# Sliding attention: TensorE's order by hand, value matmuls of both groups in pairs, modulation once a block

## Chip, cores and metric

The kernel runs on one core of a Trainium2 chip. The metric is the device time of one execution in microseconds (us). It is a whole transformer block in float32; the change touches one stage of it, 223 us of 2976.9.

## What is computed there

Group A of the token mixers is an attention over a window with a sink: 1024 queries in 8 blocks of 128, 8 query heads in 2 groups that share keys and values (width 64), a band of 384 keys around each block (256 at the two ends, and masked to a distance of 128), 256 context keys that every query sees, and one sink logit a head that takes part in the softmax and has no value.

```
def gqa_sink_attend(qb, keys, vals, bias, sink_g):
    s = jnp.einsum('bqkgd,bskd->bkgqs', qb, keys, preferred_element_type=jnp.float32) * (DH_A ** -0.5)
    if bias is not None:
        s = s + bias
    b, q = qb.shape[0], qb.shape[1]
    s_sink = jnp.broadcast_to(sink_g.astype(jnp.float32)[None, :, :, None, None], (b, KV_A, G_A, q, 1))
    p = jax.nn.softmax(jnp.concatenate([s, s_sink], axis=-1), axis=-1)[..., :-1]
    o = jnp.einsum('bkgqs,bskd->bqkgd', p.astype(vals.dtype), vals)
    return o.reshape(b, q, H_A * DH_A)
...
def modulate(h, shift, scale):
    return h * (1 + scale) + shift
```

The same stage also computes the rest of the modulation: a vector times the matrix `w_mod`, whose later columns are shift, scale and gate of the parts behind the attention. It needs nothing of the attention and is there to fill TensorE.

## The kernel before

`phase_window` (L466) loops over the 8 query blocks. `win_scores` (L499) does four heads of one group. For each head TensorE writes into one of two score buffers (`big`, two banks of PSUM each): the queries against the band's keys in two matmuls (`ks`, `kl`: the keys' high and low part), the mask as one matmul of 128 columns for each end of the band, the context keys in two matmuls, and the sink in one of two columns. VectorE then takes the negative maximum (L520), ScalarE the exponential with its sum (L522), and after four heads VectorE the four reciprocals (L525) and the scaling of the four P by them (L527).

`win_pv` (L530) does the second half for the block before. For each key tile of 128 (three of the band and two of the context; two and two at the ends) and each group it transposes the four heads' P into one bank (`t0` or `t1` in turn, L44), copies that to `PT` in SBUF (L542 on ScalarE, L544 on VectorE for one in three), and multiplies it by the values, 64 columns of the array for each group, into the accumulator `po`. Matmuls and transposes are recorded at the lines of the helpers `mm` (L41) and `tp` (L44). At the block's end ScalarE copies `po` to `oT` (L547).

`mods` is a generator over `mod_slab` (L133), for two column ranges s = 1, 2 with 16 slabs each. A slab is a load of 512 KB on SyncE's queue into `wmod` (three buffers) and four matmuls of 32 columns into four strips of one accumulator, which TensorE can run side by side. Behind a range's last slab GpSimd has cleared and loaded `bmod`, VectorE adds it (`mrows`, L154), and SyncE stores the rows (`modd`). Four slabs are asked for after each block, and at block 5 the text asks for `w_q_up`, which the next stage (`phase_up`, L549) needs: three loads of 384 KB into `wraw` (two buffers), split by a cast on ScalarE (L59) and a subtraction on VectorE (L62) into `Vb`.

Except where a block is marked with `manual_schedule`, a scheduler in the build sets the order of each engine's instructions. In this stage it does so on all engines: the text's order says what is asked for, not what stands where. It puts the loads of `w_q_up` to the front, and value matmuls, transposes and modulation between the scores as their inputs come free. An engine works its list in order; a wait holds all that is behind it.

Of the kernel before, what the change touches and what calls it, by code (L numbers as in the profile page):

```python
# [6 lines left out]
F32 = mybir.dt.float32  # L7
F32R = mybir.dt.float32r
I32 = mybir.dt.int32
U32 = mybir.dt.uint32  # L10
AF = mybir.ActivationFunctionType
ALU = mybir.AluOpType
AX = mybir.AxisListType
# [20 lines left out]
class Build:  # L34
# [205 lines left out]
    def pool(self, name, side="left", **kw):  # L240
        return self.tc.tile_pool(name=name, bufs=1, side=side, reuse_waits="tile", **kw)
# [224 lines left out]
    def phase_window(self, mods):  # L466
        nc, tc, I = self.nc, self.tc, self.I
        with self.pool("wa", "right") as wa:
            qs, ks, kl = self.qs, self.ks, self.kl
            identr, mask, ones, sink = self.win_consts  # L470
            pend = None
            for b in range(8):
                u = self.win_block(wa, b)
                self.win_scores(wa, u, 0, qs, ks, kl, identr, mask, ones, sink)
                if pend:
                    self.win_pv(wa, pend)
                self.win_scores(wa, u, 1, qs, ks, kl, identr, mask, ones, sink)
                for _ in range(4):
                    next(mods, None)
                if b == 5:  # L480
                    wq = self.vb.tile([128, 5120], F32R, name="Vb")
                    self.wq = [(wq[:, k * 1536:k * 1536 + 768], wq[:, k * 1536 + 768:k * 1536 + 1536]) for k in range(3)]
                    for k in range(3):
                        raw = wa.tile([128, 768], F32, name="wraw", bufs=2)
                        nc.sync.dma_start(raw, I["w_q_up"][k * 128:(k + 1) * 128])
                        self.split(*self.wq[k], raw)
                pend = u
            self.win_pv(wa, pend)
            for _ in mods:
                pass  # L490

    def win_block(self, wa, b):
        k0 = max(b - 1, 0)
        nb = min(b + 1, 7) - k0 + 1
        sm = self.sm
        return dict(b=b, k0=k0, nb=nb, P=[], nm=sm.tile([128, 8], F32, name="nm"),
                    sm=sm.tile([128, 8], F32, name="mmx4"))

    def win_scores(self, wa, u, g, qs, ks, kl, identr, mask, ones, sink):  # L499
        nc = self.nc  # L500
        b, k0, nb, nm, sm = u["b"], u["k0"], u["nb"], u["nm"], u["sm"]
        bw = nb * 128
        W = bw + 256
        c0 = 512 - bw
        P = []
        for h in range(g * 4, g * 4 + 4):
            ps = self.big()
            band, ctx = ps[:, c0:512], ps[:, 512:768]
            q = qs[:, h, b * 128:(b + 1) * 128]
            kb = slice(256 + k0 * 128, 256 + k0 * 128 + bw)  # L510
            self.mm(band, q, ks[:, g, kb], True, False)
            self.mm(band, q, kl[:, g, kb], False, False)
            if b:
                self.mm(ps[:, c0:c0 + 128], identr, mask[:, 0], False, b == 7)
            if b < 7:
                self.mm(ps[:, 384:512], identr, mask[:, 1], False, True)
            self.mm(ctx, q, ks[:, g, 0:256], True, False)
            self.mm(ctx, q, kl[:, g, 0:256], False, True)
            self.mm(ps[:, 768:770], ones, sink[:, h], True, True)
            nc.vector.reduce_max(nm[:, h:h + 1], ps[:, c0:770], axis=AX.X, negate=True)  # L520
            p = wa.tile([128, 656], F32, name="P", bufs=12)
            nc.scalar.activation(p[:, :W + 2], ps[:, c0:770], AF.Exp, bias=nm[:, h:h + 1], accum_out=sm[:, h:h + 1])  # L522
            P.append(p)
        ri = self.sm.tile([128, 8], F32, name="ri")[:, :4]
        nc.vector.reciprocal(ri, sm[:, g * 4:g * 4 + 4])  # L525
        for j in range(4):
            nc.vector.tensor_scalar_mul(P[j][:, :W], P[j][:, :W], ri[:, j:j + 1])  # L527
        u["P"] += P

    def win_pv(self, wa, u):  # L530
        nc = self.nc
        b, k0, nb, P = u["b"], u["k0"], u["nb"], u["P"]
        po = self.pt(3)
        kts = [2 + k0 + i for i in range(nb)] + [0, 1]
        for i, vt in enumerate(kts):
            for g in range(2):
                pt = self.pa(0, 2)
                for j in range(4):
                    self.tp(pt[:, j * 128:(j + 1) * 128], P[g * 4 + j][:, i * 128:(i + 1) * 128])
                PT = wa.tile([128, 512], F32, name="PT", bufs=5)  # L540
                if (i + g) % 3:
                    nc.scalar.copy(PT, pt)  # L542
                else:
                    nc.vector.tensor_copy(PT, pt)  # L544
                self.mm(po[g * 64:(g + 1) * 64], self.Va[:, vt, g * 64:(g + 1) * 64], PT,
                        i == 0, i == len(kts) - 1)
        nc.scalar.copy(self.oT[:, 0:4, b * 128:(b + 1) * 128], po.rearrange("p (j q) -> p j q", j=4))  # L547

    def phase_up(self):  # L549
# [1024 lines left out]
    def band_pv(self, bp, m, b, k0, nk, P):  # L1574
# [5 lines left out]
        while i < nk:  # L1580
            n2 = min(2, nk - i)
            pt = self.pa(0, 2)
            for kk in range(n2):
                for e in range(2):
                    c = kk * 256 + e * 128
                    self.tp(pt[:, c:c + 128], P[e][:, (i + kk) * 128:(i + kk + 1) * 128])
            PT = bp.tile([128, 512], F32, name="bPT", bufs=3)
            nc.scalar.copy(PT[:, :n2 * 256], pt[:, :n2 * 256])
            for kk in range(n2):
                kt = (k0 // 128) + i + kk  # L1590
                for e in range(2):
                    c = kk * 256 + e * 128
                    h = 2 * m + e
                    self.mm(po[e * 64:(e + 1) * 64], self.vb2[:, kt, h * 64:(h + 1) * 64], PT[:, c:c + 128],
                            i + kk == 0, i + kk == nk - 1)
# [214 lines left out]
    def build(self):  # L1810
        nc, tc, I = self.nc, self.tc, self.I

        pool = self.opool
        with ExitStack() as es:
            self.consts(es)
            self.dp = es.enter_context(tc.tile_pool(name="dp", bufs=1, space=DRAM))
            ek, self.cp1 = pool("cp1")
            self.krp = self.cp1
            self.modd = self.dp.tile([1, 4096], F32, name="modd")
            ehp, self.hp = pool("hp", "right")  # L1820
            ewp, self.wp = pool("wp", "right")
            self.phase_win()
            ewp.close()
            ehp.close()
            er, otp = pool("otp", "right")
            self.oT = otp.tile([128, 8, 1024], F32, name="oT")
            evb, self.vb = pool("vb", "right")
            emd, md = pool("md")

            def mods():  # L1830
                for s in (1, 2):
                    yield from self.mod_slab(md, s, self.pt(2), 3)
            self.phase_window(mods())
            emd.close()
            self.eq.close()
            self.ev.close()
            eu, self.uo = pool("uo", "right")
            self.phase_up()
            self.phase_mla()
            self.e1.close()  # L1840
            self.dbg("oT", self.oT)
            self.emk.close()
            em, self.rp = pool("rp")
            self.gf = self.rp.tile([128, 1024], F32, name="gf")
            self.phase_wout()
            eu.close()
            evb.close()
            er.close()
            self.phase_router()
            self.phase_moe()  # L1850
            self.dbg("xacc", self.xacc)
            em.close()
            ek.close()

            eh, self.hp = pool("hp2", "right")
            eb, self.bp = pool("bp")
            self.phase2_win()
            eh.close()
            for nm in ("bg", "qkvz"):
                self.dbg(nm, getattr(self, nm))  # L1860
            er, self.br = pool("br", "right")
            self.phase2_mix()
            self.dbg("oad", self.oad)
            self.ebpr.close()
            self.epre.close()
            eb.close()
            em, self.mp = pool("mp")
            e2, self.b2 = pool("b2")
            self.phase2_branch()
# [111 lines left out]
```

## Time and profile before

| | us |
|---|---|
| median of 3 runs | 2976.04 (2974.82 to 2976.28) |
| the profiled execution | 2978.69 |
| its span | 2976.9 |
| mean granted TensorE clock | 0.969 |
| first scores of the stage | 193.3 |
| first matmul of the next stage | 416.4 |

The span runs from the first instruction to the last; the profiled execution's time has another 1.8 us around it. In the rows below, PE is TensorE's matmuls, PEld its weight loads, DVE VectorE, ACT ScalarE, POOL GpSimd and SP SyncE. `t<-PT,Va` are value matmuls, `t<-wmod,ct` modulation, `t<-ident,P` transposes, `big<-...` scores. Matmuls of TensorE overlap their neighbours, so the time that one costs is the distance to the start of the next.

### The profile page before, as it was taken

What the parts mean: (1) busy time and instruction counts of PE and PEld (TensorE: products, weight loads), DVE (VectorE), ACT (ScalarE), POOL (GpSimd) and SP (SyncE); (2) the same over time, 40 slices, a digit from 0 to 9 for tenths busy, and PEclk for the clock granted to TensorE, in tenths of its full rate; (3) what the DMA queues carried; (4) which work ended last, traced back from release to release, by engine and by line L of the source; (5) the groups of instructions that cost most, each with busy time, mean ns of one, the idle gap of its engine ahead of it and who ended that gap; (6) DMA issues with size and microseconds to landing.
All of it is one profiled execution on the core that took longest, in us unless ns stands there. A gap on an engine that the chain in (4) does not pass through costs nothing. (4 is left out here: it accounts for less than half of the span.)

```text
span 2976.9 us, 36533 instructions
## 1 busy us (share of the span) xinstructions
PE 2770.0 (93%) x14180; PEld 2190.2 (74%) x14180; DVE 1774.3 (60%) x2651; ACT 1132.6 (38%) x1756; POOL 657.9 (22%) x654
## 2 busy tenths in 40 slices
PE   6999989889984999789999899999999999999997
PEld 4885556555663777578889788877898888888886
DVE  3655557777667999766437234375555445445455
ACT  4544454344324676553322223454133222222223
POOL 1000014343424887522121232030000000000000
PEclk8999999999987999899999999999999999999999
DMA  6123210001446999712453544312522111111111
GB/s 220 41 62 102 86 57 1 1 1 32 144 146 239 359 376 366 253 61 85 131 186 112 193 144 145 103 44 92 164 86 85 51 55 50 43 51 49 43 36 57
DMA packets 179981, 338.75 MB, mean 114 GB/s; under 512 B 17576, under 2 KB 104488, under 8 KB 177504
## 3 DMA queue, kind: packets, MB, share of 16 engines
q1 hardware_dynamic: 161408, 270.13, 27.2%
q0 software_dynamic: 18400, 66.28, 6.8%
q8 instruction: 112, 1.84, 0.3%
q14 instruction: 61, 0.50, 0.1%
HBM read 282.88 MB, written 53.49 MB: 113 GB/s over the span
## 5 line engine op out<-in xcount | busy, mean ns | idle before, releaser
L62 DVE TENSOR_TENSOR mlo<-mraw,mhi 128x2048 fp32r<-128x2048 f32 x63 | 222.5, 3558 | 9.3 <-ACT mhi L59 9.3
L41 PE MATMUL big<-hhi,wuhi 128*128 128x512 f32 x672 | 212.3, 393 | 0.0
L41 PE MATMUL big<-hhi,whi 128*128 128x512 f32 x656 | 210.4, 399 | 0.0
L41 PE MATMUL big<-hhi,wulo 128*128 128x512 f32 x672 | 209.5, 391 | 0.0
L41 PE MATMUL big<-hlo,wuhi 128*128 128x512 f32 x672 | 209.3, 391 | 0.0
L41 PE MATMUL big<-hlo,whi 128*128 128x512 f32 x656 | 208.5, 396 | 0.0
L41 PE MATMUL big<-hhi,wlo 128*128 128x512 f32 x656 | 207.6, 395 | 0.0
L59 ACT CAST mhi<-mraw 128x2048 fp32r<-128x2048 f32 x96 | 181.5, 1913 | 54.7 <-PE big L41 28.4
L62 POOL TENSOR_TENSOR mlo<-mraw,mhi 128x2048 fp32r<-128x2048 f32 x33 | 165.2, 5012 | 72.4 <-ACT mhi L59 68.9
L1785 DVE TENSOR_TENSOR xs<-xs,t 128x512 f32<-128x512 f32 x176 | 118.0, 686 | 83.3 <-PE t L41 83.1
L1802 POOL TENSOR_TENSOR wuraw<-wuraw,nf 128x1024 f32<-128x1024 f32 x2 | 5.2, 2622 | 723.7 <-ACT rst L100 719.0
L1744 DVE SCALAR_TENSOR_TENSOR cacc<-big,cols,cacc 128x1023 f32<-128x1023 f32 (+2 forms) x90 | 113.1, 1257 | 78.5 <-ACT cacc L1740 76.9
L62 DVE TENSOR_TENSOR wlo<-wraw,whi 128x512 fp32r<-128x512 f32 (+5 forms) x124 | 78.8, 644 | 123.8 <-ACT whi L59 122.2
L41 PEld LDWEIGHTS big<-hlo,wuhi 128*128 128x128 f32 x672 | 126.1, 188 | 28.7
L41 PEld LDWEIGHTS big<-hhi,wuhi 128*128 128x128 f32 x672 | 126.2, 188 | 27.3
L41 PEld LDWEIGHTS big<-hhi,wulo 128*128 128x128 f32 x672 | 126.2, 188 | 27.1
L782 ACT ACTIVATE P<-t 128x512 f32<-128x512 f32 x160 | 95.0, 598 | 134.2 <-PE t L41 132.9
L41 PEld LDWEIGHTS big<-hlo,whi 128*128 128x128 f32 x656 | 122.8, 189 | 26.3
L41 PEld LDWEIGHTS big<-hhi,wlo 128*128 128x128 f32 x656 | 122.8, 189 | 26.1
L41 PE MATMUL t<-wdhi,ah 128*128 128x512 f32 x352 | 137.4, 390 | 1.5 <-ACT ah L59 1.1
L41 PEld LDWEIGHTS big<-hhi,whi 128*128 128x128 f32 x656 | 121.0, 189 | 23.7
L41 PE MATMUL t<-wdlo,ah 128*128 128x512 f32 x352 | 137.3, 390 | 0.0
(606 smaller groups left out, 6931.4 us busy)
## 6 DMA issues: line engine op xcount, KB each, us to landing
mraw<-in_w_gate SPq DMA_DIRECT2D x32, 1024.0 KB, 12.6
mraw<-in_w_up SPq DMA_DIRECT2D x32, 1024.0 KB, 13.1
mraw<-in_w_down SPq DMA_DIRECT2D x32, 1024.0 KB, 9.8
wmod<-in_w_mod SPq DMA_DIRECT2D x48, 512.0 KB, 4.1
wuraw<-in_w_up SPq DMA_DIRECT2D x42, 512.0 KB, 3.9
wraw<-in_w2a SPq DMA_DIRECT2D x72, 256.0 KB, 2.8
wdraw<-in_w_down SPq DMA_DIRECT2D x22, 512.0 KB, 3.2
gxd<-gx POOLq DMA_DIRECT2D x8, 1024.0 KB, 4.7
```

The source lines that it names most:

```text
L41: self.nc.tensor.matmul(out, lhsT, rhs, start=start, stop=stop)
L59: nc.scalar.copy(hi, src)
L62: (nc.vector if lo_eng == "dve" else nc.gpsimd).tensor_sub(lo, src, hi.bitcast(F32))
L782: nc.scalar.activation(P, ps, AF.Exp, scale=self.sc_mla)
L1744: nc.vector.scalar_tensor_tensor(t[:, b:c + w], ps[:, b - tap:c + w - tap], self.col("conv_f", (2 - tap) * 44 + m), t[:, b:c + w], op0=ALU ...
L1785: nc.vector.tensor_add(xs[:, t, cs], xs[:, t, cs], ps)
L1802: nc.gpsimd.tensor_mul(y, y, nf)
```

## The change

TensorE's instructions of the stage now stand in the order of the text (`manual_schedule`). A head is a call of `win_scores`; after each one `win_pv`, now a generator, gives two steps of the block before: `turn` (four transposes and the copy to `PT` for one tile and group) or `both` (the value matmuls of both groups for one tile). The four slabs of modulation come after head 7, ahead of that block's last pair of value matmuls. The two mask matmuls of a block with both ends become one over two strips of 128 columns, ahead of `kl`, and the sink goes ahead of the context. Reciprocals are taken for two heads at a time; the even head is scaled on VectorE, the odd one on GpSimd. `P` gets 14 buffers (12 before), `PT` 4 (5), `wmod` 4 (3). `w_q_up` comes in nine pieces of 128x256 in one buffer (three of 128x768 in two).

```diff
@@ phase_window
+            with tc.manual_schedule(engines={mybir.EngineType.PE}):
+                for b in range(8):
+                    u = self.win_block(wa, b)
+                    if b == 5:
...
+                        for k in range(3):
+                            for c in range(0, 768, 256):
+                                raw = wa.tile([128, 256], F32, name="wraw")
+                                nc.sync.dma_start(raw, I["w_q_up"][k * 128:(k + 1) * 128, c:c + 256])
+                                self.split(*[w[:, c:c + 256] for w in self.wq[k]], raw)
+                    pv = self.win_pv(wa, pend) if pend else iter(())
+                    for h in range(8):
+                        self.win_scores(wa, u, h, qs, ks, kl, identr, mask, ones, sink)
+                        if h == 7:
+                            for _ in range(4):
+                                next(mods, None)
+                        for _ in range(2):
+                            next(pv, None)
+                    pend = u
+                for _ in mods:
+                    pass
+                for _ in self.win_pv(wa, pend):
+                    pass
@@ win_scores
+        self.mm(band, q, ks[:, g, kb], True, False)
+        if nb == 3:
+            self.mm(band.rearrange("p (a b) -> p a b", a=3)[:, 0:3:2], identr, mask, False, False)
+        elif b:
+            self.mm(ps[:, c0:c0 + 128], identr, mask[:, 0], False, False)
+        else:
+            self.mm(ps[:, 384:512], identr, mask[:, 1], False, False)
+        self.mm(band, q, kl[:, g, kb], False, True)
+        self.mm(ps[:, 768:770], ones, sink[:, h], True, True)
+        self.mm(ctx, q, ks[:, g, 0:256], True, False)
+        self.mm(ctx, q, kl[:, g, 0:256], False, True)
...
+        p = wa.tile([128, 656], F32, name="P", bufs=14)
...
+        if h % 2:
+            ri = self.sm.tile([128, 8], F32, name="ri", bufs=4)[:, :2]
+            nc.vector.reciprocal(ri, sm[:, h - 1:h + 1])
+            nc.vector.tensor_scalar_mul(u["P"][h - 1][:, :W], u["P"][h - 1][:, :W], ri[:, 0:1])
+            nc.gpsimd.tensor_scalar_mul(p[:, :W], p[:, :W], ri[:, 1:2])
@@ win_pv
+        def turn(i, g):
+            pt = self.pa(0, 2)
+            for j in range(4):
+                self.tp(pt[:, j * 128:(j + 1) * 128], P[g * 4 + j][:, i * 128:(i + 1) * 128])
+            t = PT[i, g] = wa.tile([128, 512], F32, name="PT", bufs=4)
+            if (i + g) % 3:
+                nc.scalar.copy(t, pt)
+            else:
+                nc.vector.tensor_copy(t, pt)
+
+        def both(i):
             for g in range(2):
...
+                self.mm(po[g * 64:(g + 1) * 64], self.Va[:, kts[i], g * 64:(g + 1) * 64], PT.pop((i, g)),
                         i == 0, i == len(kts) - 1)
+        turn(0, 0)
+        yield
+        for i in range(len(kts)):
+            turn(i, 1)
+            yield
+            if i + 1 < len(kts):
+                turn(i + 1, 0)
+                yield
+            both(i)
+            if i + 1 < len(kts):
+                yield
@@ mods
-                    yield from self.mod_slab(md, s, self.pt(2), 3)
+                    yield from self.mod_slab(md, s, self.pt(2), 4)
```

TensorE inside a block, between two heads' scores (`t_...<-PT,Va` value matmul, `t_...<-ident,P` transposes of one tile and group, `big<-` scores). Before:

```order
L44 MATMUL t_2509<-ident,P 128x128 x4
L41 MATMUL t_2484<-PT,Va 64x512 x2
L44 MATMUL t_2517<-ident,P 128x128 x4
L44 MATMUL t_2525<-ident,P 128x128 x4
L41 MATMUL big<-ks,qs 128x384
L41 MATMUL big<-kl,qs 128x384
L41 MATMUL t_2484<-PT,Va 64x512
L44 MATMUL t_2533<-ident,P 128x128 x4
L41 MATMUL big<-mask,identr 128x128 x2
L41 MATMUL big<-ks,qs 128x256
L41 MATMUL big<-kl,qs 128x256
```

After:

```order
L44 MATMUL t_2471<-ident,P 128x128 x4
L41 MATMUL t_2442<-PT,Va 64x512 x2
L41 MATMUL big<-ks,qs 128x384
L41 MATMUL big<-mask,identr 128x2x128
L41 MATMUL big<-kl,qs 128x384
L41 MATMUL big<-sink,onesr 128x2
L41 MATMUL big<-ks,qs 128x256
L41 MATMUL big<-kl,qs 128x256
L44 MATMUL t_2490<-ident,P 128x128 x4
L44 MATMUL t_2497<-ident,P 128x128 x4
```

The value matmuls, which stood alone or in twos and sometimes inside a head's scores, now stand in twos between whole heads, with at least one head between a pair and the transposes that it needs last.

TensorE around the modulation of the same block (`t_2007` or `t_2013` is its accumulator). Before:

```order
L41 MATMUL t_2484<-PT,Va 64x512
L44 MATMUL t_2493<-ident,P 128x128 x4
L44 MATMUL t_2501<-ident,P 128x128 x4
L41 MATMUL t_2007<-wmod,ct 32x256 x4
L41 MATMUL big<-ks,qs 128x384
```

After:

```order
L41 MATMUL big<-ks,qs 128x256
L41 MATMUL big<-kl,qs 128x256
L41 MATMUL t_2013<-wmod,ct 32x256 x16
L41 MATMUL t_2442<-PT,Va 64x512 x2
L41 MATMUL big<-ks,qs 128x384
L41 MATMUL big<-mask,identr 128x2x128
```

Before, a block's modulation is spread in groups of 1 to 12 matmuls over it; now all 16 stand in one place, ahead of the block's last two value matmuls.

SyncE's loads and ScalarE's work at the start of the stage (`Vb<-wraw` is the cast of a piece of `w_q_up`). SyncE before:

```order
L139 DMA wmod<-in_w_mod 128x4x256 x3
L485 DMA wraw<-in_w_q_up 128x768 x2
L139 DMA wmod<-in_w_mod 128x4x256 x3
L485 DMA wraw<-in_w_q_up 128x768
L139 DMA wmod<-in_w_mod 128x4x256 x12
```

SyncE after:

```order
L139 DMA wmod<-in_w_mod 128x4x256 x4
L482 DMA wraw<-in_w_q_up 128x256 x3
L139 DMA wmod<-in_w_mod 128x4x256 x4
L482 DMA wraw<-in_w_q_up 128x256 x2
L139 DMA wmod<-in_w_mod 128x4x256 x4
L482 DMA wraw<-in_w_q_up 128x256 x3
L139 DMA wmod<-in_w_mod 128x4x256 x4
L482 DMA wraw<-in_w_q_up 128x256
L139 DMA wmod<-in_w_mod 128x4x256 x2
```

ScalarE before:

```order
L522 ACTIVATE P,mmx_1914<-big,nm 128x514 x2
L59 CAST Vb<-wraw 128x768 x2
L522 ACTIVATE P,mmx_1914<-big,nm 128x514 x5
L59 CAST Vb<-wraw 128x768
L522 ACTIVATE P,mmx_1914<-big,nm 128x514
L522 ACTIVATE P,mmx_2033<-big,nm 128x642
```

ScalarE after:

```order
L529 ACTIVATE P,mmx_1916<-big,nm 128x514 x2
L59 CAST Vb<-wraw 128x256
L529 ACTIVATE P,mmx_1916<-big,nm 128x514 x2
L59 CAST Vb<-wraw 128x256
L529 ACTIVATE P,mmx_1916<-big,nm 128x514 x3
L59 CAST Vb<-wraw 128x256
L529 ACTIVATE P,mmx_1916<-big,nm 128x514
L529 ACTIVATE P,mmx_2039<-big,nm 128x642
```

The loads of `w_q_up` go between groups of four slabs, and the casts, all three in the first block before, are spread over several blocks.

## Rows read from the trace of the kernel before

**Rows 1.** The page, part 1: busy us of each engine (share of the span), xinstructions.

```profile
PE 2770.0 (93%) x14180; PEld 2190.2 (74%) x14180; DVE 1774.3 (60%) x2651; ACT 1132.6 (38%) x1756; POOL 657.9 (22%) x654
```

**Rows 2.** Windows: length, busy us of PE PEld DVE ACT POOL (xinstructions), clock, DMA.

```profile
193.00:221.00 28.00, 23.82 (x147) 22.64 (x149) 5.87 (x20) 9.57 (x24) 2.48 (x5) 0.94 0.24 78
221.00:245.00 24.00, 22.20 (x160) 13.83 (x150) 15.92 (x30) 14.55 (x32) 0.00 (x0) 1.00 0.58 178
...
320.00:345.00 25.00, 24.47 (x149) 14.49 (x148) 12.32 (x22) 11.06 (x25) 0.00 (x0) 1.00 0.27 85
...
395.00:416.00 21.00, 17.83 (x92) 8.66 (x89) 6.51 (x12) 8.30 (x18) 0.56 (x1) 1.00 0.28 101
```

**Rows 3.** Timeline of PE, fourth block: start, busy us, operation, xrecords [idle before <-releaser].

```profile
269.77 1.58 PE L41 MATMUL t<-PT,Va 128*64 128x512 f32 x4
271.28 1.09 PE L44 MATMUL t<-ident,P 128*128 128x128 f32 x8
...
274.90 0.16 PE L41 MATMUL big<-sink,onesr 128*128 128x2 f32 x1
274.92 0.42 PE L41 MATMUL big<-ks,qs 128*128 128x384 f32 x1
...
282.93 1.09 PE L44 MATMUL t<-ident,P 128*128 128x128 f32 x8
283.95 0.64 PE L41 MATMUL t<-wmod,ct 128*32 128x256 f32 x8
284.52 0.44 PE L41 MATMUL big<-ks,qs 128*128 128x384 f32 x1
...
284.97 0.34 PE L41 MATMUL big<-mask,identr 128*128 128x128 f32 x2
285.14 0.33 PE L41 MATMUL big<-ks,qs 128*128 128x256 f32 x1
...
285.43 0.17 PE L41 MATMUL big<-sink,onesr 128*128 128x2 f32 x1
285.52 1.07 PE L41 MATMUL t<-PT,Va 128*64 128x512 f32 x2
286.53 0.66 PE L44 MATMUL t<-ident,P 128*128 128x128 f32 x4
287.11 1.87 PE L41 MATMUL t<-PT,Va 128*64 128x512 f32 x4
288.92 1.09 PE L44 MATMUL t<-ident,P 128*128 128x128 f32 x8
289.77 0.42 PE L41 MATMUL big<-ks,qs 128*128 128x384 f32 x1
```

**Rows 4.** Timeline of PE, start of the modulation.

```profile
220.42 1.07 PE L41 MATMUL t<-wmod,ct 128*32 128x256 f32 x16 [1.50 <-ACT cqT L405]
```

**Rows 5.** Lines, 193 to 416 us: xcount | busy us, mean ns | idle before, releasers.

```profile
L41 PE MATMUL t<-PT,Va 128*64 128x512 f32 x152 | 69.7, 617 | 4.3 <-ACT PT L542 2.9 <-DVE ri L525 0.9 <-DVE PT L544 0.4
...
L520 DVE TENSOR_REDUCE nm<-big 128x1 f32<-128x642 f32 x48 | 39.1, 824 | 54.1 <-PE big L41 53.2
L522 ACT ACTIVATE P<-big,nm 128x642 f32<-128x642 f32 x48 | 38.3, 799 | 36.1 <-DVE nm L520 28.7 <-PE t L44 7.1
...
L41 PE MATMUL t<-wmod,ct 128*32 128x256 f32 x256 | 25.2, 389 | 3.1 <-DMA wmod<-in_w_mod 1.6 <-ACT cqT L405 1.5
...
L527 DVE TENSOR_SCALAR P<-P,ri 128x640 f32<-128x640 f32 x48 | 23.3, 548 | 0.2
```

**Rows 6.** Lines, GpSimd, whole span.

```profile
L787 POOL TENSOR_TENSOR acc<-P 128x512 f32<-128x512 f32 x8 | 10.3, 1286 | 19.1 <-ACT P L782 19.0
```

**Rows 7.** Tile bP, another softmax's P: duration ns min/median/max, first and last start.

```profile
L1570 DVE TENSOR_SCALAR bP<-bP,mm x64: 285/553/2630, 1905.7 to 2048.6; 128x640 f32<-128x640 f32 x32, 128x128 f32<-128x128 f32 x8, 128x256 f32<-128x256 f32 x8, 128x384 f32<-128x384 f32 x8
```

**Rows 8.** The page's DMA issues: xcount, KB each, median us to landing.

```profile
wmod<-in_w_mod SPq DMA_DIRECT2D x48, 512.0 KB, 4.1
...
wraw<-in_w_q_up SPq DMA_DIRECT2D x3, 384.0 KB, 8.2
```

More of the change, by code (lines that the diff above doesn't have):

```diff
@@ L471, in phase_window @@
             pend = None
[L472 to L490, printed above, removed]
+            with tc.manual_schedule(engines={mybir.EngineType.PE}):
+                for b in range(8):
+                    u = self.win_block(wa, b)
+                    if b == 5:
+                        wq = self.vb.tile([128, 5120], F32R, name="Vb")
+                        self.wq = [(wq[:, k * 1536:k * 1536 + 768], wq[:, k * 1536 + 768:k * 1536 + 1536])
+                                   for k in range(3)]
+                        for k in range(3):
[16 more added lines that the diff above has]
+                    pass
     def win_block(self, wa, b):
@@ L497, in win_block, with win_scores @@
                     sm=sm.tile([128, 8], F32, name="mmx4"))
-    def win_scores(self, wa, u, g, qs, ks, kl, identr, mask, ones, sink):
+    def win_scores(self, wa, u, h, qs, ks, kl, identr, mask, ones, sink):
         nc = self.nc
@@ L504, in win_scores @@
         c0 = 512 - bw
[L505 to L528, printed above, removed]
+        g = h // 4
+        ps = self.big()
+        band, ctx = ps[:, c0:512], ps[:, 512:768]
+        q = qs[:, h, b * 128:(b + 1) * 128]
+        kb = slice(256 + k0 * 128, 256 + k0 * 128 + bw)
+        self.mm(band, q, ks[:, g, kb], True, False)
@@ new lines, in win_scores @@
+        nc.vector.reduce_max(nm[:, h:h + 1], ps[:, c0:770], axis=AX.X, negate=True)
+        p = wa.tile([128, 656], F32, name="P", bufs=14)
+        nc.scalar.activation(p[:, :W + 2], ps[:, c0:770], AF.Exp, bias=nm[:, h:h + 1], accum_out=sm[:, h:h + 1])
+        u["P"].append(p)
+        if h % 2:
[3 more added lines that the diff above has]
+            nc.gpsimd.tensor_scalar_mul(p[:, :W], p[:, :W], ri[:, 1:2])
@@ L534, in win_pv @@
         kts = [2 + k0 + i for i in range(nb)] + [0, 1]
-        for i, vt in enumerate(kts):
-            for g in range(2):
[L537 to L545, printed above, removed]
-                        i == 0, i == len(kts) - 1)
+        PT = {}
+        def turn(i, g):
[8 more added lines that the diff above has]
+        def both(i):
+            for g in range(2):
+                self.mm(po[g * 64:(g + 1) * 64], self.Va[:, kts[i], g * 64:(g + 1) * 64], PT.pop((i, g)),
+                        i == 0, i == len(kts) - 1)
+        turn(0, 0)
[9 more added lines that the diff above has]
+                yield
         nc.scalar.copy(self.oT[:, 0:4, b * 128:(b + 1) * 128], po.rearrange("p (j q) -> p j q", j=4))
```

## The prediction, as it was made before the result

> **What bounds the kernel now.** I read the engines' shares first: TensorE is busy 93% of the span [rows 1]. So the stage that the diff touches, the sliding attention, was cut into stretches next [rows 2]. Inside a block TensorE is busy 24.47 of 25 us at clock 1.00, VectorE 12.32 and ScalarE 11.06, GpSimd nothing: there TensorE's own work sets the pace, and the others have half of the time to spare. Two stretches differ: the first block (22.20 of 24) and the last one, which has no scores of a next block to fill with (17.83 of 21).
>
> "Busy" hides how well TensorE is used, so the third view is its own sequence. There I read the distance from one start to the next, not the durations, since neighbours overlap. (Each value or modulation matmul leaves two records, so x2 is one value matmul, x8 one slab of four.) A value matmul alone takes 285.52 to 286.53, 1.01 us; two together, one for each group, 269.77 to 271.28, 1.51 us, so .75 each [rows 3]. One round of modulation (four matmuls of 32 columns side by side) takes 283.95 to 284.52, .57 us; two rounds in one group are busy 1.07 where one is busy .64 [rows 3, 4], so a further round costs .43, and .14 falls on each group whatever its size. The time that can be had is therefore in how TensorE's work is grouped, not in its waits: those before the value matmuls are 4.3 us in the whole stage and before the modulation 3.1 [rows 5].
>
> **The change, part by part.** All in us of the profiled execution, which took 2978.69; that is 2.65 above the median of 2976.04, so the forecast for the median is 2.65 below the sum.
>
> *Value matmuls.* The orders of the two programs give 32 alone and 22 pairs before, 38 pairs after. 32 x 1.01 + 22 x 1.51 = 65.5 becomes 38 x 1.51 = 57.4: **-8.1**. TensorE is the bound here, so all of it is on the path.
>
> *Modulation.* Before, 128 matmuls stand in 28 groups of 1 to 12, 43 rounds when each group is rounded up to fours; after, 8 groups of 16, 32 rounds. 43 x .43 + 28 x .14 = 22.4 becomes 32 x .43 + 8 x .14 = 14.9: **-7.5**. Four slabs in four buffers must be there at a block's end; they are loaded during the block before, some 20 us ahead, so I cost the loads at nothing. If that cover failed it would show as a wait like the 1.6 us that the modulation row has now [rows 5].
>
> *Mask.* Two matmuls become one of the same columns: .17 for the two (284.97 to 285.14) [rows 3]. One can cost between .085 and .17: 0 to -4.1 over 48 heads; I take .05 off each, **-2.4**.
>
> *Changes of kind of work.* Eight transposes before a modulation group take 1.02 (282.93 to 283.95), before scores .85 (288.92 to 289.77): .17 more. The order loses all 17 such places and gains 8 from transposes to a value matmul, for which I take the same .17. From the sink to a value matmul it is .09 (285.43), to the next head .02 (274.90) [rows 3], with 28 such places fewer. -2.9 + 1.4 - 2.0 = **-3.5**.
>
> *Idle TensorE.* The blocks leave .5 of 25 us, the last stretch 3.2 [rows 2], the value matmuls wait 4.3 [rows 5]. In the new order a pair has a whole head of scores (some .9 us) or more between its last transposes and itself. A pair that came right behind its transposes took 1.81 (287.11 to 288.92) and not 1.51 [rows 3]. I take half of the 7 us: **-3.5**, bounds 0 and -7.
>
> *First block.* No transposes or modulation now stand between block 0's scores, so the two score buffers set the pace: scores .9 (284.52 to 285.43 [rows 3]), maximum .82, exponential .80 [rows 5]; (.9 + .82 + .80) / 2 = 1.26 a head where TensorE needs .9. Eight heads leave **+2.9** idle; hand-overs would add to it, this block's shorter rows (512 keys, not 640) take from it. The granted clock is .94 in the stretch where TensorE was busy 23.82 of 28 [rows 2], so it falls when TensorE has gaps; if the new gaps bring the lower level (1.2 GHz) for part of this block, its 7 us of scores stretch by 0 to 7: **+2.5**.
>
> *GpSimd's half of the scaling.* 32 multiplications by 1/sum leave VectorE (548 ns each [rows 5]) for GpSimd. The trace shows none there: not under 548, and by the addition over 128x512 (1286 [rows 6]) up to 1.6 us for 640 columns. I take 1.2, near that row, since it is GpSimd's own. VectorE falls to about 10.5 of 20.5 us a block even with two more reciprocals, and ScalarE's 11 stays. Head 7's chain is the tightest: .82 + .80 + 1.2 = 2.8 and the hand-overs from its scores to a scaled P, while modulation (1.9), the last pair (1.5), the next block's first scores (.9) and four transposes (.4) stand ahead of the transpose that reads it, 4.7. So it is **0**, with 1.9 to spare for hand-overs; at 1.6 us still 1.5.
> GpSimd's cost to VectorE is another matter: the same scaling on VectorE in a later stage, where GpSimd has work too, runs 285 to 2630 ns around a median of 553 [rows 7]. The Trainium skill, "SBUF — State Buffer", section "Who interferes with whom", says why: a tensor_scalar of VectorE may take the port pair that it shares with GpSimd, and whoever holds it blocks the other for the whole instruction. By that rule this part speaks against the change; the 2630 agrees with it. At worst each of 32 scalings on VectorE stands 2.1 us longer, four a block: 10.5 + 8.4 = 18.9, still under 20.5, so the sum stays.
>
> *Loads of w_q_up.* Three of 384 KB (8.2 us to land) become nine of 128 KB in a single buffer, between the slabs' loads (4.1) [rows 8]; their casts stand among the exponentials in ScalarE's order. I cost them at **0**: the first two blocks' exponentials leave ScalarE half idle. If a load is late, its cast holds up all behind it (below).
>
> Sum: -8.1 - 7.5 - 2.4 - 3.5 - 3.5 + 2.9 + 2.5 = **-19.6**. 2978.69 - 19.6 = 2959.1, less 2.65 is **2956.4**. A later block then takes about 20.5 to 21.5 us. Nothing outside the stage moves in any engine's order.
>
> **The rivals.** 0.2%, 6 us, is about what a measurement of this kernel can tell from no change.
>
> *Slower: ScalarE stands at the casts.* Nine casts wait for pieces in one buffer, each behind up to four slabs on the loading queue; exponentials and copies stand behind them, and with a fixed order TensorE cannot go around. For it: the single buffer. Against: before, three casts stood in the same place and no wait of TensorE is put down to them [rows 5]. Each wait that reaches TensorE comes nine times at most; it eats the gain from 19.6 / 9 = 2.2 us each, and at the 8.2 us of [rows 8] for half of them it is 37 - 20 = 17 slower, 2993. Chance .05.
>
> *No change: the fixed order waits as much as it saves.* The scheduler's order bent around late copies; a fixed one stops. If the pairs and transposes each time wait some .45 for a copy that VectorE is late with, 38 x .45 = 17 comes back: 2973. It needs VectorE standing longer than [rows 7] shows typically. Chance .08.
>
> *Half of the gain.* All 38 pairs cost 1.81 [rows 3]: +11.4, so -8.4, 2967.6. Chance .12.
>
> *More.* Two value matmuls of 64 columns run wholly side by side when they stand together: 1.01 a pair, 38 x .5 = 19 more, 2937. The pairs of before speak against: 1.51 [rows 3]. The Trainium skill, "TensorEngine Tiling (Array Packing)", section "Theoretical Speedup", gives up to 2x for 64 columns or fewer; the 1.51 is 1.34 times. Chance .03.
>
> **How the numbers follow.** The forecast, a gain of 13 to 28, has .72; its own range is 2948 to 2963 (mask +-2, idle +-3.5, first block and clock -5 to +5). With half of the gain (.12) and more (.03) faster is .87; same .08; slower .05. The range takes in the smaller gain and half of the larger: 2944 to 2970, leaving out .16.
>
> **What would show it.** Right: value matmuls only in pairs, 1.5 apart; modulation in eight groups of 1.9; copies to `oT` 20.5 to 21.5 apart from the second to the seventh; TensorE busy over 24 of 25 us from the second block on; the later phases begin about 20 us earlier; GpSimd 32 scalings of .5 to 1.6 us. The first block should show more idle TensorE than before. Wrong: TensorE waiting for `PT` at most pairs (then the copies, not TensorE, are the bound); ScalarE idle ahead of a cast for longer than 2 us, with TensorE behind it; scalings on VectorE well over 2 us on most heads; or pairs that do not stay at 1.51.

## The result, and the profile after

The changed kernel takes 2930.34 us (median of 4 runs, 2930.09 to 2934.21) where the kernel before took 2976.16 (4 runs, 2974.82 to 2979.70): a ratio of 0.9847, 95% interval 0.9830 to 0.9864, so 45.8 us less. I had forecast 2956.4, a gain of 20, in a range of 2944 to 2970: the sign was right, the forecast gain was less than half of the real one, and the time lies outside the range. The profiled execution took 2934.21 us (span 2932.4), 44.5 less than the one before.

I measure the stage from its last projection matmul (211.39 us in the changed kernel, 212.94 before) to the first matmul of the next stage (378.38, 416.35). That is **167.0 us where it was 203.4: 36.4 less**. The other 8 of the 44.5 lie outside the stage.

The windows of the changed kernel (length, then busy us of PE, PEld, DVE, ACT, POOL, then the clock), to set beside [rows 2]; a block now takes some 19 us:

```profile
217.00:236.00 19.00, 14.59 (x82) 10.90 (x81) 8.12 (x18) 10.14 (x23) 7.49 (x4) 0.63 0.33 105
236.00:255.00 19.00, 18.64 (x132) 12.51 (x130) 12.28 (x23) 10.66 (x24) 7.43 (x4) 1.00 0.38 121
275.00:295.00 20.00, 20.00 (x150) 14.14 (x149) 12.74 (x23) 12.38 (x28) 9.60 (x7) 1.00 0.34 116
...
355.00:378.00 23.00, 22.06 (x144) 11.82 (x143) 8.98 (x17) 10.81 (x24) 6.30 (x5) 1.00 0.25 94
```

In the fourth block (275 to 295) TensorE is busy without a gap, 20.00 of 20; behind a wait at 256 us, in the third block, none of its waits shows until the next stage. In block 0 (217 to 236) it stands at a granted clock of 0.63 and is busy 14.59 of 19 us.

The lines of the stage (count | busy us, mean ns of one | idle before them, and what ended it), to set beside [rows 5] and [rows 6]:

```profile
L535 POOL TENSOR_SCALAR P<-P,ri 128x640 f32<-128x640 f32 x24 | 50.6, 2108 | 62.3 <-DVE ri L533 57.5 <-DMA wmod<-in_w_mod 4.8
L41 PE MATMUL t<-PT,Va 128*64 128x512 f32 x152 | 44.7, 618 | 0.0
L44 PE MATMUL t<-ident,P 128*128 128x128 f32 x304 | 43.8, 277 | 1.4 <-POOL P L535 1.2
...
L41 PE MATMUL t<-wmod,ct 128*32 128x256 f32 x256 | 17.2, 414 | 0.0
...
L534 DVE TENSOR_SCALAR P<-P,ri 128x640 f32<-128x640 f32 x24 | 13.2, 550 | 0.6
```

The value matmuls fell from 69.7 us busy to 44.7 for the same 152 records, and their idle time from 4.3 to 0. GpSimd takes 2108 ns for a scaling, more than any row before suggested.

TensorE's timeline (start, busy us, operation, records), to set beside [rows 3]:

```profile
276.18 1.27 PE L41 MATMUL t<-PT,Va 128*64 128x512 f32 x4
277.37 0.44 PE L41 MATMUL big<-ks,qs 128*128 128x384 f32 x1
...
279.09 0.42 PE L41 MATMUL big<-ks,qs 128*128 128x384 f32 x1
...
280.09 1.08 PE L41 MATMUL t<-PT,Va 128*64 128x512 f32 x4
281.10 0.66 PE L44 MATMUL t<-ident,P 128*128 128x128 f32 x4
...
283.95 0.44 PE L41 MATMUL big<-ks,qs 128*128 128x384 f32 x1
...
284.87 1.03 PE L44 MATMUL t<-ident,P 128*128 128x128 f32 x8
...
289.05 1.93 PE L41 MATMUL t<-wmod,ct 128*32 128x256 f32 x32
290.92 1.08 PE L41 MATMUL t<-PT,Va 128*64 128x512 f32 x4
```

Here the two value matmuls of a pair take **1.01 us together** (280.09 to 281.10), as long as one alone took before. The pair at 276.18 takes 1.19. In the kernel before I had read 1.51 and 1.81. A head still takes .92 ahead of transposes (283.95 to 284.87) and 1.00 ahead of value matmuls (279.09 to 280.09; 284.52 to 285.52 in [rows 3]), and four slabs take 1.87 (289.05 to 290.92).

What the forecast missed was in the trace of the kernel before, in blocks that I had not read. Two other groups of four records there:

```profile
241.17 1.08 PE L41 MATMUL t<-PT,Va 128*64 128x512 f32 x4
242.18 1.09 PE L44 MATMUL t<-ident,P 128*128 128x128 f32 x8
...
263.17 1.46 PE L41 MATMUL t<-PT,Va 128*64 128x512 f32 x4
264.57 1.09 PE L44 MATMUL t<-ident,P 128*128 128x128 f32 x8
```

One pair takes 1.01 (241.17 to 242.18) and one 1.40. So the 1.51 of [rows 3] was not the price of a pair, but of a pair whose second matmul got its `PT` late. The copies show it. Beside the pair of [rows 3] that takes 1.51 (from 269.77), the second copy on ScalarE and the pair's second matmul by itself:

```profile
269.64 0.59 ACT L542 COPY PT<-t 128x512 f32<-128x512 f32 x1 [3.74 <-PE big L41]
```

```profile
270.28 1.07 PE L41 MATMUL t<-PT,Va 128*64 128x512 f32 x2
```

The copy ends at 270.23, .46 behind the start of the pair; the second matmul starts at 270.28 and takes 1.00. In the changed kernel both copies of the pair at 280.09 have ended by 280.06:

```profile
278.99 1.07 ACT L551 COPY PT<-t 128x512 f32<-128x512 f32 x2 [1.27 <-PE t L44]
```

In 21 of the 22 pairs of the kernel before, the second copy ends .26 to .75 us behind the start of the pair and the second matmul starts some .05 behind that; in the one that takes 1.01 both copies had ended before it began.

### The profile page after: what moved, and what is told of

It is laid out like the page before. It is cut to its first block, busy times and chain, and to the rows that moved or that the text cites. A ratio compares the mean times of both kernels' runs of the same rounds, so it can differ in the third digit from the quotient of the medians.

```text
span 2932.4 us, 36530 instructions
## 1 busy us (share of the span) xinstructions
PE 2726.3 (93%) x14132; PEld 2183.9 (74%) x14132; DVE 1765.5 (60%) x2641; ACT 1133.0 (39%) x1762; POOL 722.2 (25%) x686
## 5 line engine op out<-in xcount | busy, mean ns | idle before, releaser
L62 POOL TENSOR_TENSOR mlo<-mraw,mhi 128x2048 fp32r<-128x2048 f32 x33 | 165.5, 5022 | 74.9 <-ACT mhi L59 74.1
```

The source lines that it names most:

```text
L62: (nc.vector if lo_eng == "dve" else nc.gpsimd).tensor_sub(lo, src, hi.bitcast(F32))
```

## Experiments

Stage lengths below are measured as above, changed kernel 167.0, before 203.4. Executions of one kernel differ by 4 to 12 us, so single times are given only where they help; the stage's length is steadier: 159.8 and 161.0 in two traces of one and the same kernel. Differences of under some 1.5 us therefore say nothing.

### Is the pair's time the cause? Pairs taken apart

```diff
             if i + 1 < len(kts):
+                one(i, 0)
                 turn(i + 1, 0)
                 yield
-            both(i)
-            if i + 1 < len(kts):
+                one(i, 1)
                 yield
+            else:
+                one(i, 0)
+                one(i, 1)
```

`one(i, g)` is the value matmul of one group, half of `both`.

> 30 of the 38 pairs of value matmuls are taken apart: the next four transposes stand between the two. All else as in the changed kernel, whose pairs take 1.01 us and whose next stage begins at 378.1 us. Theory A (two value matmuls run wholly side by side when the second one's copy is there in time): the 30 become 60 matmuls of 1.0, so about 30 x 1.0 = 30 us longer: next stage at 405 to 412, time 2957 to 2965. Rival B (a pair is worth only the 0.5 us that I forecast, and the rest of the gain is elsewhere): 15 us longer, next stage at about 393, time about 2945.

Measured: stage 199.8 us, next stage at 414.0 (378.4 in the changed kernel), time 2966.69, both just beyond Theory A's ranges. Its value matmuls on TensorE's timeline:

```profile
299.62 1.07 PE L41 MATMUL t<-PT,Va 128*64 128x512 f32 x2
300.62 0.66 PE L44 MATMUL t<-ident,P 128*128 128x128 f32 x4
...
302.03 1.07 PE L41 MATMUL t<-PT,Va 128*64 128x512 f32 x2
303.04 0.65 PE L44 MATMUL t<-ident,P 128*128 128x128 f32 x4
```

Each alone takes 1.00 and 1.01 again. 30 pairs taken apart cost 32.8 us, a little over one matmul each: 28.1 in the value matmuls, most of the rest in transposes (3.1) and scores (1.4), which now change places with other work more often. Theory A holds, B falls. This is what 30 pairs are worth against single matmuls. The kernel before had 22 late pairs already; from there to the changed kernel the value matmuls went from 66.0 to 42.1 us (start to start, waits left out), 23.9 of the stage's 36.4.

### Does standing together suffice? Pairs right behind their transposes

```diff
-        turn(0, 0)
-        yield
         for i in range(len(kts)):
+            turn(i, 0)
             turn(i, 1)
-            yield
...
             both(i)
```

In `phase_window` one step of it follows each head, not two.

> The value matmuls stay in pairs, but each pair stands right behind its eight transposes, without a head of scores between. Theory A (how far the two overlap is set by how late the second copy is): the pairs start with 0.3 to 0.5 us between the two and take 1.3 to 1.8, and TensorE also waits before them; at 38 x (0.5 + about 0.4) some 25 to 40 us longer, next stage at 403 to 418. Rival C (standing next to each other in the order is enough, and in the kernel before something else kept them apart): the pairs take 1.0 after a wait; only the waits show, 38 x 0.4 = 15 us, next stage at about 393.

Measured: stage 225.6 us, time 2995.03, slower than before the change. On TensorE's timeline:

```profile
301.68 1.03 PE L44 MATMUL t<-ident,P 128*128 128x128 f32 x8
303.36 1.93 PE L41 MATMUL t<-PT,Va 128*64 128x512 f32 x4 [0.64 <-DVE PT L552]
305.21 0.44 PE L41 MATMUL big<-ks,qs 128*128 128x384 f32 x1
```

The second copy of this pair, on ScalarE:

```profile
303.58 0.58 ACT L550 COPY PT<-t 128x512 f32<-128x512 f32 x1
```

The eight transposes end near 302.7; the pair waits .64 for a copy of VectorE's and then takes 1.85 (303.36 to 305.21), as the copy on ScalarE ends at 304.16. No pair of the first four blocks took under 1.5. So the order of the two instructions is not enough: how much of the second matmul lies beside the first is set by when its operand arrives. Rival C falls. The cost, 58.6 us, went beyond my 25 to 40: the value matmuls take 27.5 longer, the waits ahead of them 13.6, and the rest falls on transposes and on the waits ahead of transposes and scores, for which I had nothing.

### Is it the order by hand? The scheduler's order with the changed text

```diff
-            with tc.manual_schedule(engines={mybir.EngineType.PE}):
+            if True:
```

> TensorE's order is given back to the scheduler; text, buffers, mask, scaling and loads stay as changed. In its order 800 rows into the program the value matmuls mostly stand in pairs with a head between them and their transposes. Theory A: the pairs are what counts, so it keeps most of the gain: next stage at 380 to 388, time 2932 to 2942. Rival D (the fixed order itself is what gains): it falls back to the neighbourhood of the kernel before, next stage beyond 400.

Measured: stage 167.3 us, time 2934.52. The scheduler, given the new text, makes 35 pairs and 6 single ones by itself, most of them at 1.01. Theory A holds (next stage at 381.6), Rival D falls. The .3 us between the two orders are within what two traces of one kernel differ by, so the fixed order by itself shows no gain: what counts is that the text asks for both groups' matmuls together, a step after their transposes. The larger numbers of buffers, the smaller pieces of `w_q_up` and the grouping of the modulation have no run of their own.

### What lies outside the stage? 64 bytes

In the last stage the same matmuls were longer before than after, with the same order on every engine. The one difference that I found there is where tensors lie: the change gives `ri` four buffers of 32 bytes in place of two, in a pool that stands ahead of nearly everything in SBUF, so all that follows moves up by 64 bytes. Two kernels move only that. First the kernel before with four buffers:

```diff
-        ri = self.sm.tile([128, 8], F32, name="ri")[:, :4]
+        ri = self.sm.tile([128, 8], F32, name="ri", bufs=4)[:, :4]
```

> The kernel before with four buffers of `ri` instead of two and nothing else: every engine's order is the same, but all that lies behind in SBUF moves up by 64 bytes, as it does in the changed kernel. In the traces the changed kernel's stage is 36.4 us shorter, yet the medians are 45.8 apart, and in the last stage the same matmuls stand 0.2294 us apart before and 0.2267 after. Theory G (where the tensors lie sets that): the last stage runs at 0.227 and the time falls by 5 to 9 us, to 2967 to 2971. Rival H (one execution differs from another): the time stays within 2 us of the kernel before, 2974 to 2978, and the distance varies by itself.

Then the changed kernel with two:

```diff
-            ri = self.sm.tile([128, 8], F32, name="ri", bufs=4)[:, :2]
+            ri = self.sm.tile([128, 8], F32, name="ri")[:, :2]
```

> The changed kernel with `ri` back at two buffers, all engines' orders the same, so that everything behind lies where it lay before. Theory G: the stage stays at 167 us, the last stage goes back to 0.229 us a matmul, and the time rises by 5 to 9 us over the changed kernel's 2930.3, to 2935 to 2939. Rival H: 2929 to 2932.

Measured: the kernel before falls to 2965.66 (5 runs) beside 2977.66 (9 runs), a ratio of 0.9963, interval 0.9950 to 0.9977, some 11 us, with its stage still 203.6. The changed kernel without the 64 bytes takes 2936.48 (4 runs), 6 more, with its stage at 165.5; but its ratio to the kernel before, 0.9863 (0.9848 to 0.9878), overlaps the changed kernel's 0.9847 (0.9830 to 0.9864). The lines of the last stage's matmuls on the page (count | busy us, mean ns), kernel before:

```profile
L41 PE MATMUL big<-hhi,wuhi 128*128 128x512 f32 x672 | 212.3, 393 | 0.0
...
L41 PE MATMUL big<-hhi,wulo 128*128 128x512 f32 x672 | 209.5, 391 | 0.0
L41 PE MATMUL big<-hlo,wuhi 128*128 128x512 f32 x672 | 209.3, 391 | 0.0
```

The kernel before with the 64 bytes:

```profile
L41 PE MATMUL big<-hhi,wuhi 128*128 128x512 f32 x672 | 209.7, 389 | 0.0
...
L41 PE MATMUL big<-hlo,wuhi 128*128 128x512 f32 x672 | 208.2, 389 | 0.0
L41 PE MATMUL big<-hhi,wulo 128*128 128x512 f32 x672 | 208.2, 389 | 0.0
```

The changed kernel without them:

```profile
L41 PE MATMUL big<-hhi,wuhi 128*128 128x512 f32 x672 | 212.3, 393 | 0.0
...
L41 PE MATMUL big<-hhi,wulo 128*128 128x512 f32 x672 | 209.4, 391 | 0.0
L41 PE MATMUL big<-hlo,wuhi 128*128 128x512 f32 x672 | 209.3, 391 | 0.0
```

In the changed kernel all three are at 389. So three groups lose 5.0 us of 631.1 with the shift, and get them back without it, whichever order the attention has. From the first to the last of these matmuls it is 680.4 us in the two kernels without the 64 bytes and 676.3 to 676.4 in the twelve with them. For this stage, 4.1 us, Theory G holds. The median of the kernel before fell by more (12 us, clear of noise). Where the rest lies stays open: from the start of the next stage to the end the twelve take 2548.4 to 2557.4 us and the two 2560.6 and 2556.0, so single traces can't tell it from what executions differ by. What about the addresses it is stays open too.

### The mask and the sink

```diff
-        self.mm(ps[:, 768:770], ones, sink[:, h], True, True)
         self.mm(ctx, q, ks[:, g, 0:256], True, False)
         self.mm(ctx, q, kl[:, g, 0:256], False, True)
+        self.mm(ps[:, 768:770], ones, sink[:, h], True, True)
```

> The sink matmul of every head goes back behind the context, the merged mask stays. In the changed kernel a head takes 0.92 us as before, so the merged mask, which I priced at -0.05 a head, shows no gain. Theory J (the mask does gain 0.05 a head, and the sink between band and context takes it back): 0.03 to 0.06 a head less, 64 heads, the stage 2 to 4 us shorter than its 167.0. Rival K (the merged mask gains nothing): within 0.7 us.

Measured: stage 163.2 us, 3.8 less. A head on TensorE's timeline, from `ks` to what follows the sink:

```profile
276.84 0.42 PE L41 MATMUL big<-ks,qs 128*128 128x384 f32 x1
...
277.62 0.17 PE L41 MATMUL big<-sink,onesr 128*128 128x2 f32 x1
277.71 0.65 PE L41 MATMUL t<-PT,Va 128*64 128x512 f32 x2
```

That is .87 where a head ahead of a value matmul takes 1.00 in the changed kernel (279.09 to 280.09) and in the one before. Over all such heads the medians are .88, .99 and 1.00, ahead of transposes .84, .92 and .92. The transposes get 1.9 us longer in all, so the stage gains 3.8 and not 6. Theory J holds: with the sink in its old place the merged mask, which now also stands ahead of `kl`, makes a head shorter by more than the .05 that I priced, and the sink between band and context took it back. A kernel with the two old masks in the new order was not run.

### GpSimd's share

```diff
-            nc.gpsimd.tensor_scalar_mul(p[:, :W], p[:, :W], ri[:, 1:2])
+            nc.vector.tensor_scalar_mul(p[:, :W], p[:, :W], ri[:, 1:2])
```

> The odd heads' scaling goes back from GpSimd to VectorE. On GpSimd one takes 2.1 us in the changed kernel (I had 1.2, up to 1.6) and TensorE waited for it once, 1.2 us. Theory L (it lies beside TensorE's work, VectorE has the room): the stage changes by -2 to +1 us from 167.0. Rival M (VectorE's share matters): over 3 us longer, with TensorE waiting for VectorE's P or PT.

Measured: stage 166.7 us, .3 less, within what two traces of one kernel differ by. Theory L holds: this part of the change neither gains nor costs anything that shows.

### Block 0 and the clock

First a slab of modulation after every second head of block 0:

```diff
-                        if h == 7:
+                        if b == 0 and h % 2:
+                            next(mods, None)
+                        if b and h == 7:
```

> Only in block 0, one slab of modulation after every second head in place of four at its end. In the changed kernel the granted clock falls to 0.5 in that block (0.63 in the stretch from 217 to 236 us) and four slabs take 3.6 us there where they take 1.9 later. Theory E (TensorE's gaps between the lone scores of block 0 bring the lower clock): with the gaps filled the clock stays at 1.00 or falls for a shorter time, and the next stage begins 3 to 6 us earlier, at 372 to 375. Rival F (the clock falls because of the gap of some 6 us before block 0, whatever stands in it): the clock falls as before and the gain is below 1.5 us.

Measured: stage 167.7 us, no gain; the granted clock was 0.55 from 217 to 236, lower than without. From the third head on TensorE had no gap there, and stayed at the lower level:

```profile
222.50:233.50 11.00, 11.00 (x59) 7.89 (x59) 6.61 (x13) 4.50 (x12) 5.04 (x3) 0.50 0.50 157
```

So Theory E falls, and Rival F looked right, for this filling. The clock falls ahead of block 0, not in it, in the kernel before as in the changed one. TensorE waits some 2.5 us there (for `clo`), and is at the lower level behind that wait. In the changed kernel:

```profile
214.00:217.00 3.00, 2.28 (x11) 2.31 (x12) 1.52 (x5) 0.00 (x0) 0.39 (x1) 0.51 1.04 353
```

In the kernel before, which is back at 1.00 by 220 us (by 226 in its trace with the 64 bytes, in the same order):

```profile
216.00:218.00 2.00, 1.87 (x9) 1.90 (x10) 0.97 (x3) 0.00 (x0) 0.00 (x0) 0.50 1.07 353
...
220.00:222.00 2.00, 1.14 (x20) 0.49 (x24) 0.00 (x0) 1.97 (x3) 0.00 (x0) 1.00 0.73 273
```

The changed kernel's own block 0 shows what the low clock costs:

```profile
221.10 0.58 PE L41 MATMUL big<-ks,qs 128*128 128x256 f32 x1 [3.59 <-ACT P L529]
...
231.01 3.64 PE L41 MATMUL t<-wmod,ct 128*32 128x256 f32 x32
234.58 0.44 PE L41 MATMUL big<-ks,qs 128*128 128x384 f32 x1
```

The four slabs take 3.57 (231.01 to 234.58) where later ones take 1.87. The wait of 3.59 ahead of the third head is for the first exponential. ScalarE had copies of `cqT` to make from 217.13 on and then loaded a table:

```profile
218.98 1.28 ACT L529 ACT_TABLE_LOAD   x1
220.27 0.69 ACT L529 ACTIVATE P<-big,nm 128x514 f32<-128x514 f32 x1
```

In the kernel before modulation stood in that wait (220.42 in [rows 4]). In the run with the scheduler's order three slabs stood behind the second head, and TensorE was back at full speed some 10 us earlier. So the next try put three there and one behind the fifth head (with the sink last):

```diff
-                        if h == 7:
-                            for _ in range(4):
-                                next(mods, None)
+                        for _ in range({(0, 1): 3, (0, 4): 1}.get((b, h), 4 if b and h == 7 else 0)):
+                            next(mods, None)
```

> The changed kernel with the sink last (stage 163.2 us by the trace), and in block 0 three slabs of modulation behind the second head and one behind the fifth in place of four at the end, where TensorE otherwise waits some 3.6 us for the first exponentials. Theory E2 (a slab a pair of heads came too late; the gap before the third head is what holds the lower clock): the clock is back at 1.00 by some 225 us, as where the scheduler put three slabs there, and the stage is 2 to 4 us shorter, 159 to 161. Rival F (nothing that stands in block 0 changes it): within 1 us of 163.2.

Measured: stage 159.8 us, 3.4 less than with the sink alone, clock 0.84 from 217 to 236:

```profile
219.07 2.79 PE L41 MATMUL t<-wmod,ct 128*32 128x256 f32 x24 [1.51 <-ACT cqT L405]
221.79 0.58 PE L41 MATMUL big<-ks,qs 128*128 128x256 f32 x1
...
224.83 0.38 PE L41 MATMUL big<-ks,qs 128*128 128x256 f32 x1 [0.91 <-ACT P L528]
...
226.18 0.38 PE L41 MATMUL big<-ks,qs 128*128 128x256 f32 x1
```

The three slabs still run at the lower level (2.72 us), and from the fourth head on the matmuls are at full speed again: `ks` of 256 columns is busy .38 where it was .58. E2 is borne out in size, though the slabs also fill the wait of 3.6 us, and no run tells this part of the 3.4 from the clock's; why slabs in front bring the clock back, and slabs between the heads do not, these runs do not tell.

### The last pairs, and both together

Three of the last block's slabs go between the last transposes and pairs; in the second kernel with the filled block 0:

```diff
-                            for _ in range(4):
+                            for _ in range(4 if b < 7 else 1):
...
-                for _ in self.win_pv(wa, pend):
-                    pass
+                for n, _ in enumerate(self.win_pv(wa, pend)):
+                    if n in (2, 5, 8):
+                        next(mods, None)
...
```

> The changed kernel with the sink last, and three of the last block's slabs moved between transposes and value matmuls behind the loop, where the last four pairs start 0.36 to 0.8 us apart because they stand right behind their transposes. Theory A: the slabs give the second copy its time, three pairs go from 1.06, 1.37, 1.49 to about 1.0 us, so the stage is 0.5 to 1.5 us shorter than 163.2. Rival N: the slabs only take up room there, and end later: no gain, or the next stage waits for the modulation's rows, up to 2 us longer.

> Sink last, three slabs behind the second head and one behind the fifth of block 0, three slabs of the last block among the last pairs. If the parts add: stage 158 to 163 us in place of 167.0, and the time 4 to 9 us below the changed kernel's 2930.3, 2921 to 2927. Rival: the parts other than the sink give nothing, 2926 to 2928.

Measured: stage 163.1 us, .1 less than without, though three of the last pairs did go to 1.01. The trace tells why. From the last block's modulation to the next stage it is 15.1 us (360.67 to 375.77) where the kernel without this takes 14.5 (359.19 to 373.73). With one slab in place of four ahead of the last transposes, TensorE comes to a P that GpSimd hasn't scaled yet:

```profile
364.65 0.76 PE L44 MATMUL t<-ident,P 128*128 128x128 f32 x5 [1.10 <-POOL P L537]
```

So Rival N holds: the pairs gain .9, and this wait and the split modulation (four groups of .57 for one of 1.86) take more. Both together: stage 161.0 us, 2927.59 (4 runs, just beyond the range for parts that add and inside the rival's), ratio 0.9851 (0.9822 to 0.9879); the last 15.1 us are as long as in the run before, so of the two only the filled block 0 gains. The kernel with sink last and block 0 filled, timed by itself:

> The kernel of the run with sink last and block 0 filled again, timed in five rounds (its stage 159.8 us, one time 2925.5). If the stage alone decides, 7 us below the changed kernel's 2930.3: 2922 to 2927. If the differences between executions in the later stages are as large, 2926 to 2932.

Measured: 2925.95 us (5 runs, 2921.31 to 2932.43), a ratio of 0.9829 to the kernel before, interval 0.9815 to 0.9844; its stage took 161.0 us in this execution, 159.8 in the one before. That is the lowest median of all, 4.4 below the changed kernel, but the two intervals overlap: the trace shows the shorter stage, the times alone don't separate the two.

## Why the prediction was wrong

**The step that failed is the first term**, value matmuls at 38 x 1.51 = 57.4. 28 of the 38 pairs take 1.01, and all of them together 42.1. (The first pair of five blocks takes 1.2, one 2.1, and the last four, with no heads between, 1.06 to 1.9.) From start to start, waits left out, the value matmuls went from 66.0 to 42.1, 23.9 us less in place of 8.1. The rival "More" (two of 64 columns run wholly side by side, 1.01 a pair) was the right one, and I gave it .03, since [rows 3] shows pairs at 1.51. I took the distance of a pair as a property of the pair. It held a wait that the idle column doesn't show, as TensorE was busy with the first matmul while the second one's operand was on its way: in the kernel before, the second `PT` copy ended .26 to .75 us behind the start of 21 of the 22 pairs. I had seen that a pair right behind its transposes takes 1.81 and not 1.51, and didn't ask whether the 1.51 had a wait in it as well. Splitting the pairs (+32.8) and making their operands late (+58.6) show both halves of it. The Trainium skill, "TensorEngine Tiling (Array Packing)", section "Theoretical Speedup", says up to 2x for 64 columns; the traces agree, 2 x 1.00 against 1.01, for pairs whose operands are there.

Counted like this, the stage's 36.4 are, to a tenth, 23.9 of value matmuls, 6.6 of modulation (forecast 7.5), and 6.0 of transposes (2.7), scores (.2) and waits (3.1), for which mask, changes of kind, idle time, first block and clock together came to 4.0. That this last sum came near is in part luck, as the next paragraphs show: of its terms the mask and the first block were not as I had them.

**Modulation**, forecast at 14.9 us: seven groups at 1.87 and one at 3.57, 16.7. At full clock eight groups would take 15.0, so the price was right, and the difference belongs to the clock.

**Mask**, -2.4: a head is as long as before (.92 ahead of transposes, 1.00 and .99 ahead of value matmuls), net 0. I priced the mask and left the sink's move at nothing, without a reason; with the sink last the stage is 3.8 shorter.

**First block**, +2.9 idle and +2.5 clock: that it would lose time was right, the way was not. The even pace of the two score buffers, 1.26 a head, shows as three waits of .32, .32 and .18. The bulk, 3.59, is one wait for the first exponential, behind ScalarE's other work, for which the sum had no term. And the gaps of block 0 didn't bring the lower clock: it had fallen ahead of the block, as in the kernel before, and stayed, so that a head there takes 1.45 (221.10 to 222.55), longer than the pace that I had worked out. Three slabs ahead of the third head gave 3.4 us back.

**Idle time**, -3.5: the waits ahead of value matmuls (4.3) and modulation (3.1) went to 0; those ahead of transposes are 1.4 now, and those ahead of the stage's scores 4.4, all of it block 0's, where they were 1.4.

**GpSimd**: 2108 ns a scaling where I took 1200 and at most 1600. No row of the kernel before had that operation, and an addition over 512 columns was a poor stand-in. It cost nothing, since the slack of 1.5 to 1.9 us that I had worked out was enough but for one wait of 1.2. The rule of the Trainium skill ("SBUF — State Buffer", section "Who interferes with whom") threatened VectorE; VectorE's scalings stayed at 550 ns against 548. Of GpSimd's, one that began just behind VectorE's scaling (272.37 and 272.31) took 2.24 us, one that began beside a maximum 1.88: what the sharing can have cost, some .3 or .4 by these two (an estimate; no run takes it by itself), fell on GpSimd, which had time for it.

**"Nothing outside the stage moves in any engine's order"** was true, and I took it to mean that nothing outside changes. Addresses did: 4.1 us in the last stage, in every trace, and 12 us in the median of the kernel before.

The rival "Half of the gain" has a slip: 19.6 less 11.4 is 8.2, not 8.4, so 2967.8. Nothing hangs on it.

Of the 44.5 us between the two profiled executions, then, 36.4 lie in the stage, two thirds of it in the pairs, and 4.1 in the last stage, by where tensors lie. The other 4 lie elsewhere and can't be told from what executions differ by.

## What to carry to other kernels

Before you price a pair of matmuls by the distance to the next instruction, read several pairs: where they differ (here 1.01, 1.40, 1.51, 1.81), compare the end of the second operand's copy with the start of the pair. Here the shortest was the price, and the rest a wait that no idle column shows, because the engine is busy with the first. Let a whole unit of other work stand between the transposes and the matmuls that use their copies (here a head of .9 us, enough for 28 of 38 pairs). And when a change adds even a small buffer ahead of others, time a kernel that moves only the addresses before you credit the gain to the change.

## What was not expected of the hardware

- Shifting nearly all of SBUF by 64 bytes changed three groups of matmuls from 393, 391, 391 ns to 389 each, the last stage by 4.1 us, and the median of the kernel before by 12 us.
- Block 0 stayed at the lower clock for some 13 us in the changed kernel, and some 16 us when its gaps were filled with single slabs, though TensorE was busy 11.00 of 11 us; but it came back some 10 us earlier when three slabs stood together ahead of the third head.
